# A decoder trunk's last product: one fixed order for the weight steps of VectorE, other rooms for raw tiles, differences and x2, and output copied out by ScalarE

## The chip, the cores and the metric

The kernel runs on one core of one Trainium2 chip. The metric is the device time of one execution in microseconds (us); lower is better. Times are given as the median over several runs. A profiled execution gives the trace that is read here.

## The reference, cut to what matters

One layer of a decoder, 256 tokens, width 2048, all in f32. The part that the change touches is the end: a SwiGLU feed-forward network (FFN) and the residual.

```python
D_MODEL, SEQ, D_FF = 2048, 256, 5632

def swiglu(h, w_ffn_in, w_ffn_out):
    gate, up = jnp.split(h @ w_ffn_in, 2, axis=-1)
    return (jax.nn.silu(gate) * up) @ w_ffn_out

def reference(x, c, ...):
    ...
    x = x + gate1 * mixing_sublayer(h, ...)          # attention and linear attention branches
    h = rms_norm(x, norm2_gain[l]) * (1 + scale2) + shift2
    x = x + gate2 * swiglu(h, w_ffn_in[l], w_ffn_out[l])
    return x
```

## The kernel before, in words

**Tiles and halves.** The 256 tokens are two token tiles of 128. A weight matrix is cut into column blocks of 512 and, along the summed dimension, into chunks of 128. A *raw tile* is two chunks of one column block: 128 x 1024 f32, 512 KB, loaded by one DMA on SyncE's queue (SP), line 159. To multiply f32 exactly enough, each raw tile is taken apart by `halve`: ScalarE (ACT) casts it to the rounded type, `whi` (line 166), and VectorE (DVE) takes the rest, `wlo` = raw - `whi` (line 167). Activations are kept as two halves too. TensorE (PE) then does three matmuls for one product (`mm3`): high by high (line 170), activation's high by `wlo` (171), activation's low by `whi` (172). `whi` and `wlo` each have a ring of four rooms, so a cast can run at most four tiles ahead of TensorE.

**Rooms for raw tiles.** `raw_tile` goes round a ring: four rooms of the pool tag `raw`, and after them the tags named in `rooms["extra"]`, which are places that other data held earlier. In the FFN these are A4 and A8; in the last product H4 to H7. H0 to H3 and H4 to H7 hold the two halves of the FFN's input activation h2.

**Stages.** The FFN's input product has eleven column blocks of gate and of up. The first is plain. In the ten others (and in the last product) `paired` works on two column blocks at once: over the first `4 n` chunks the 2 x 2 arrangement of token tiles and column blocks is computed with seven products instead of eight, by sums of activations (prepared in `h2_sums` or `act_sums`) and differences of raw tiles. With r0 and r1 the two column blocks of one half of the chunks, r2 and r3 those of the other half, the differences are

- t1 = r1 - r0, t2 = r3 - t1, t3 = r3 - r1, t4 = r2 - t2,

made by VectorE in `differ` (line 1230). Each raw tile or difference that is used is then taken to halves and multiplied: r0, t1, t2, r2, t3 first (six matmuls each, `product`), and after them "rest" tiles of plain products (twelve matmuls each) by turns with r3 and t4. Two additions of VectorE (line 1252) put partial sums together. The FFN's blocks have n = 1, the last product has n = 2 (two of each difference). The differences live in A13 and A14 (FFN), and in A13, A14, H2, H3 (last product).

**The last product** has four column blocks of the output, `w_ffn_out`, in the order of n = 0 to 3. At n = 0 and n = 2 `paired` computes two of them nearly to their end (the first and the third pass); n = 1 and n = 3 finish the second one. `add_out` then multiplies the PSUM tile by gate2 (line 1343), adds x2, the residual (line 1345), and stores. x2 is loaded back from DRAM into A2, A3, A4, A8 (line 1331).

**What sets the order.** The program is written once through, and a scheduler orders the instructions of each engine. Work inside `prio()` counts as if it stood several thousand places earlier, so loads, casts, low halves and differences are taken as early as the scheduler's own reckoning lets them. `tc.issue_after(x)` makes it keep an instruction behind x. Until now the differences had no such tie: `state["split"]` held the last low half only and served the running sums of `gate2` (`mac`). On the chip each engine then works through its list in order. The PSUM pool `acc` has four banks, all taken by a pair.

After an up block, VectorE multiplies silu(gate) by up (line 1319, two steps), and TensorE transposes the result (line 1071) during a later block.

## Time and profile before

| what | value |
|---|---|
| median of 3 runs | 1624.76 us (1622.45 to 1627.54) |
| profiled execution | 1626.09 us, span of its instructions 1624.3 us |
| TensorE busy | 1592.4 us, 98% of the span |
| VectorE busy | 1242.4 us, 76% |
| ScalarE busy | 855.2 us, 53% |
| FFN's input product, blocks 2 to 11 | about 936 to 1369 us of the span |
| last product | from 1369 us |
| mean granted clock of TensorE | 0.995 |

How to read the rows: a timeline row has the start in us, the duration in us, the engine, the line, the operation, output<-input by the program's names without buffer numbers, partitions x elements and type, and the count of merged instructions; in brackets the idle time of that engine before the row and what ended it. A row of a stretch has its bounds, its length, the busy time of PE, weight loads, DVE, ACT and POOL with their counts, the granted clock (1.00 is full), the busy share of the DMA engines, and GB/s. A row of the DMA list has output<-input, queue, operation, count, size, and the median us from issue to landing. TensorE's matmul records overlap, since a matmul starts before the one ahead has drained; the distance of two starts is what one costs.

### The profile page before, as it was taken

The page shows a single profiled execution, that of the slowest core. Times are in us where ns is not written, and L with a number is a line of the kernel's source. Part 1 is how long each engine was busy: PE and PEld are TensorE (multiplying, and loading weights), DVE is VectorE, ACT ScalarE, POOL GpSimd, SP SyncE. Part 2 cuts the span into 40 slices and gives each one's busy share as a digit, 9 for nine tenths or more (in the row PEclk, how much of TensorE's full clock was granted, in tenths as well). Part 3 has the DMA queues.
Part 4 walks back from the last instruction along what each step waited for, and adds up shares of the span by engine and source line. Part 5 has one row for each costly group of instructions (what it writes and reads, how often), then busy time and mean ns, then how long its engine had stood idle before and what let it go on. Part 6 is the DMA issues. An engine that isn't in the chain of part 4 may idle for free.

```text
span 1624.3 us, 20044 instructions
## 1 busy us (share of the span) xinstructions
PE 1592.4 (98%) x7269; PEld 1311.2 (81%) x7269; DVE 1242.4 (76%) x1418; ACT 855.2 (53%) x1180; POOL 5.4 (0%) x14
## 2 busy tenths in 40 slices
PE   8999999999999999999999999999999998999999
PEld 7878888788777888888887888888888886788787
DVE  6889995877779787878657788888888875755754
ACT  5654449756587444444445555555555553534432
POOL 1000000000000000000000000000000000000000
PEclk9999999999999999999999999999999999999999
DMA  8999997874767888888776577777776666665653
GB/s 325 354 326 323 325 312 224 281 267 136 249 231 233 265 305 311 314 289 314 236 219 226 161 252 253 259 254 252 245 232 194 185 190 224 206 200 178 211 154 114
DMA packets 116179, 399.24 MB, mean 246 GB/s; under 512 B 13090, under 2 KB 13896, under 8 KB 116080
## 3 DMA queue, kind: packets, MB, share of 16 engines
q1 hardware_dynamic: 115856, 397.95, 74.0%
q8 instruction: 57, 0.93, 0.2%
q14 instruction: 42, 0.34, 0.1%
q0 software_dynamic: 224, 0.01, 0.0%
HBM read 393.71 MB, written 4.19 MB: 245 GB/s over the span
## 4 chain that ended last, share of the span: by engine, by line
PE 89%; DVE 4%; DMA 3%; ACT 2%; issue 1%; POOL 0%; DVEq 0%; ACTq 0%; POOLq 0%
PE acc L172 27%; PE acc L171 27%; PE acc L170 27%; DVE wlo L167 2%; ACT whi L166 1%; PE misc L1071 1%; DMA H<-w_ffn_out 1%; PE acc L430 1%; DMA AR<-ada_rest 1%; PE misc L786 1%; DMA raw<-w_ffn_out 1%; PE misc L170 1%; PE misc L171 1%; PE misc L172 1%; DMA raw<-w_in 0%
## 5 line engine op out<-in xcount | busy, mean ns | idle before, releaser
L166 ACT CAST whi<-raw 128x1024 fp32r<-128x1024 f32 (+1 forms) x449 | 459.4, 1028 | 483.1 <-PE acc L172 365.0
L167 DVE TENSOR_TENSOR wlo<-raw,whi 128x1024 fp32r<-128x1024 f32 (+1 forms) x449 | 531.1, 1191 | 223.0 <-ACT whi L166 219.2
L170 PE MATMUL acc<-whi,H 128*128 128x512 f32 x1476 | 578.7, 392 | 0.8 <-ACT H L442 0.4
L171 PE MATMUL acc<-wlo,H 128*128 128x512 f32 x1476 | 578.0, 392 | 1.1 <-DVE wlo L167 1.0
L172 PE MATMUL acc<-whi,H 128*128 128x512 f32 x1476 | 578.1, 392 | 1.0 <-DVE H L1157 0.6
L172 PEld LDWEIGHTS acc<-whi,H 128*128 128x128 f32 x1476 | 278.1, 189 | 59.8 <-DVE H L449 1.8
L170 PEld LDWEIGHTS acc<-whi,H 128*128 128x128 f32 x1476 | 278.1, 188 | 58.3 <-ACT H L442 1.3
L171 PEld LDWEIGHTS acc<-wlo,H 128*128 128x128 f32 x1476 | 278.1, 188 | 58.0 <-DVE wlo L167 2.2
L166 ACT CAST whi<-A 128x1024 fp32r<-128x1024 f32 x98 | 103.0, 1054 | 89.1 <-PE acc L172 85.5
L167 DVE TENSOR_TENSOR wlo<-A,whi 128x1024 fp32r<-128x1024 f32 x98 | 118.7, 1221 | 30.8 <-ACT whi L166 29.9
L170 PE MATMUL acc<-whi,A 128*128 128x512 f32 x332 | 130.5, 393 | 6.7 <-ACT whi L166 6.7
L171 PE MATMUL acc<-wlo,A 128*128 128x512 f32 x332 | 129.8, 391 | 0.0
L172 PE MATMUL acc<-whi,A 128*128 128x512 f32 x312 | 122.0, 391 | 0.0
L287 DVE SCALAR_TENSOR_TENSOR ada<-AR,csil,ada 128x1024 f32<-128x1024 f32 x59 | 75.1, 1279 | 6.8 <-DMA AR<-ada_rest 6.8
L170 PEld LDWEIGHTS acc<-whi,A 128*128 128x128 f32 x332 | 62.6, 188 | 20.6 <-ACT whi L166 7.7
L166 ACT CAST whi<-H 128x1024 fp32r<-128x1024 f32 x41 | 43.0, 1053 | 63.7 <-PE acc L172 40.4
L167 DVE TENSOR_TENSOR wlo<-H,whi 128x1024 fp32r<-128x1024 f32 x41 | 49.9, 1223 | 34.2 <-ACT whi L166 29.2
L171 PEld LDWEIGHTS acc<-wlo,A 128*128 128x128 f32 x332 | 62.6, 188 | 13.4 <-DVE wlo L167 0.4
L172 PEld LDWEIGHTS acc<-whi,A 128*128 128x128 f32 x312 | 58.8, 189 | 12.1
L170 PE MATMUL acc<-whi,T 128*128 128x512 f32 x120 | 46.8, 390 | 0.0
L172 PE MATMUL acc<-whi,T 128*128 128x512 f32 x120 | 46.7, 389 | 0.0
L171 PE MATMUL acc<-wlo,T 128*128 128x512 f32 x120 | 46.7, 389 | 0.0
(402 smaller groups left out, 1556.7 us busy)
## 6 DMA issues: line engine op xcount, KB each, us to landing
raw<-w_in SPq DMA_DIRECT2D x203, 512.0 KB, 4.9
raw<-w_ffn_in SPq DMA_DIRECT2D x122, 512.0 KB, 4.5
AR<-ada_rest SPq DMA_DIRECT2D x79, 512.0 KB, 4.8
A<-w_ffn_in SPq DMA_DIRECT2D x54, 512.0 KB, 4.4
raw<-w_ffn_out SPq DMA_DIRECT2D x53, 512.0 KB, 4.3
H<-w_ffn_out SPq DMA_DIRECT2D x35, 512.0 KB, 4.5
raw<-w_out SPq DMA_DIRECT2D x32, 512.0 KB, 4.5
KC<-ada_rest SPq DMA_DIRECT2D x30, 512.0 KB, 5.3
```

The source lines that it names most:

```text
L166: nc.scalar.copy(hi, raw)
L167: state["split"] = nc.vector.tensor_tensor(lo, raw, hi.bitcast(F32), op=ALU.subtract)
L170: nc.tensor.matmul(ps, lh, rh, start=start, stop=False, skip_group_check=seeded)
L171: nc.tensor.matmul(ps, lh, rl, start=False, stop=False, skip_group_check=seeded)
L172: state["mm"] = nc.tensor.matmul(ps, ll, rh, start=False, stop=stop, skip_group_check=seeded)
L287: nc.vector.scalar_tensor_tensor(acc, raw, c, acc, op0=ALU.mult, op1=ALU.add)
L430: state["warm"] = nc.tensor.matmul(ps, ones_r, wide, start=True, stop=True)
L786: nc.tensor.matmul(ps[:n, t * N_GLA + h, :].rearrange("p (s l) -> p s l", l=L), at(f, h, t)[:, :n], odd(at(f, h, t)), start=True, stop=True,)
L1071: nc.tensor.transpose(ps[:, i, :], src[:, i * P : (i + 1) * P], ident)
```

## The change

1. `halve` and `differ` both go through a new `in_order`. Once `state["ordered"]` is set, each low half and each difference of VectorE is kept behind the one written ahead of it. The switch is set after the first column block of the FFN's input product (i = 0). `paired` writes its steps in another order: t1, r0, then t1's halves and t2 by turns, t2's halves, r2's halves and t3 by turns, t3's halves; t4 stands ahead of the rest tile that follows it. Raw tiles are asked for with all r0 first, then r1, r2, r3.
2. In the last product the extra rooms are A4 and A8, with H2 and H3 for the third pass; differences live in A13, A14, A2, A3; x2 in H4 to H7; the last tiles' halves in H2 to H5, A2, A3.
3. After the second and third pass (n = 1 and 2) ScalarE copies the two PSUM tiles to H4 (`kept`), and `add_out` reads the copy, without `prio()`.

```diff
--- before.py
+++ after.py
@@ -164,7 +164,12 @@
 
     def halve(hi, lo, raw):
         nc.scalar.copy(hi, raw)
-        state["split"] = nc.vector.tensor_tensor(lo, raw, hi.bitcast(F32), op=ALU.subtract)
+        state["split"] = in_order(lo, raw, hi.bitcast(F32), op=ALU.subtract)
+
+    def in_order(*args, **kw):
+
+        with tc.issue_after(state["split"].ins) if "ordered" in state else nullcontext():
+            return nc.vector.tensor_tensor(*args, **kw)
 
     def mm3(ps, lh, ll, rh, rl, start, stop, seeded=False):
         nc.tensor.matmul(ps, lh, rh, start=start, stop=False, skip_group_check=seeded)
@@ -1227,25 +1232,33 @@
 
         def differ(x, y, tag=None, into=None):
             d = S(tag, [P, 2, NB]) if into is None else into
-            nc.vector.tensor_tensor(d, x, y, op=ALU.subtract)
+            state["split"] = in_order(d, x, y, op=ALU.subtract)
             return d
 
         with prio():
-            raws = [(raw_tile(src, 4 * g, b0), raw_tile(src, 4 * g, b1)) for g in range(n)]
-            raws = [r + (raw_tile(src, 4 * g + 2, b0), raw_tile(src, 4 * g + 2, b1)) for g, r in enumerate(raws)]
+            raws = {(c, b, g): raw_tile(src, 4 * g + c, b) for c, b in ((0, b0), (0, b1), (2, b0), (2, b1)) for g in range(n)}
+            raws = [[raws[c, b, g] for c in (0, 2) for b in (b0, b1)] for g in range(n)]
+            t1 = [differ(r[1], r[0], p[0]) for p, r in zip(places, raws)]
             first = [halved(r[0]) for r in raws]
-            t1 = [differ(r[1], r[0], p[0]) for p, r in zip(places, raws)]
-            first += [halved(t) for t in t1]
-            t2 = [differ(r[3], t, p[1]) for p, r, t in zip(places, raws, t1)]
+            t2 = []
+            for p, r, t in zip(places, raws, t1):
+                first.append(halved(t))
+                t2.append(differ(r[3], t, p[1]))
             first += [halved(t) for t in t2]
-            first += [halved(r[2]) for r in raws]
-            first += [halved(differ(r[3], r[1], p[0])) for p, r in zip(places, raws)]
+            t3 = []
+            for p, r in zip(places, raws):
+                first.append(halved(r[2]))
+                t3.append(differ(r[3], r[1], p[0]))
+            first += [halved(t) for t in t3]
         rest = []
         for q in range(2 * n):
             g, k = q % n, 4 * n + 2 * q
+            if q < n:
+                with prio():
+                    differ(raws[g][2], t2[g], into=t2[g])
             w = load_weights(src, k, k + 2, b0)
             with prio():
-                rest.append((w, halved(raws[g][3] if q < n else differ(raws[g][2], t2[g], into=t2[g]))))
+                rest.append((w, halved(raws[g][3] if q < n else t2[g])))
 
         def add(dst):
             with prio(2 * AHEAD):
@@ -1310,6 +1323,7 @@
             block(pu, h2_at, w_ff, 0, KC, NFF)
             h2_sums = [left_sums(("A2", "A3"), ("A13", "A14"), h2[0][0], h2[1][0])]
             rooms["extra"] = ("A4", "A8")
+            state["ordered"] = True
         else:
             block(pu, h2_at, w_ff, 4, KC, NFF + i, go_on=True, seeded=True)
         hi = S(ftags[2 * i], [P, 4, T], F32R)
@@ -1324,10 +1338,9 @@
 
         later.append(turn)
         act.append((hi, lo))
-    rooms["extra"] = ()
     x2 = []
     for n in range(4):
-        xr = S(("A2", "A3", "A4", "A8")[n], [P, NT, NB])
+        xr = S(f"H{4 + n}", [P, NT, NB])
         nc.sync.dma_start(xr, x2_far[:, n])
         x2.append(xr)
 
@@ -1352,14 +1365,14 @@
     K0 = 4 * len(act_sums)
     for n in range(4):
         if n % 2 == 0:
-            rooms["extra"] = ("H4", "H5", "H6", "H7")
+            rooms["extra"] = ("A4", "A8", "H2", "H3")[: 2 + n]
             both = [[acc_bank() for _ in range(NT)] for _ in range(2)]
-            paired(act_at, act_sums, [("A13", "A14"), ("H2", "H3")], w_fo, n, n + 1, *both, KF)
+            paired(act_at, act_sums, [("A13", "A14"), ("A2", "A3")], w_fo, n, n + 1, *both, KF)
         pss = both[n % 2]
         if n == 3:
             rooms["extra"] = ()
             block(pss, act_at, w_fo, K0, CUT, n, more=True, go_on=True, seeded=True)
-            w = load_weights(w_fo, CUT, KF, n, spare=[f"H{j}" for j in range(2, 8)])
+            w = load_weights(w_fo, CUT, KF, n, spare=("H2", "H3", "H4", "H5", "A2", "A3"))
             block(pss, act_at, None, CUT, KF, 0, w=w, tiles=(0,), go_on=True, seeded=True)
             with prio():
                 add_out(n, 0, pss[0])
@@ -1381,9 +1394,16 @@
             if n == 0:
                 flush()
                 gate2 = state["gate2"]
+                with prio():
+                    for t in range(NT):
+                        add_out(n, t, pss[t])
+                continue
+            kept = S("H4", [P, NT, NB])
             with prio():
                 for t in range(NT):
-                    add_out(n, t, pss[t])
+                    nc.scalar.copy(kept[:, t, :], pss[t])
+            for t in range(NT):
+                add_out(n, t, kept[:, t, :])
 
 
 _INS = ["x", "c", "b_ada", "norm1_gain", "norm2_gain", "sb_q_gain", "sb_k_gain", "dil_q_gain", "dil_k_gain", "w_gla_a",
```

Line 167 (the low half) and 1230 (the difference) are both line 172 in the new text; 170 to 172 become 175 to 177, 1252 becomes 1265, 1319 becomes 1333, 1331 becomes 1344.

**VectorE in the first paired block of the FFN.** raw_1722 is r0, A4_1723 r1, A8_1724 r2, raw_1725 r3; A13 holds t1 and later t3, A14 t2 and later t4; raw_1739 is the first rest tile. Before:

```order
L167 TENSOR_TENSOR wlo_1727_8093<-raw_1722_8084,whi_1726_8092 128x1024
L167 TENSOR_TENSOR wlo_1730_8099<-A13_1728_8096,whi_1729_8098 128x1024
L1230 TENSOR_TENSOR A13_1736_8112<-raw_1725_8090,A4_1723_8086 128x1024
L167 TENSOR_TENSOR wlo_1733_8105<-A14_1731_8102,whi_1732_8104 128x1024
L1319 TENSOR_TENSOR scr_1680_7908<-scr_1680_7908,acc_1678_7906 128x512
L1319 TENSOR_TENSOR scr_1681_7910<-scr_1681_7910,acc_1679_7907 128x512
L1230 TENSOR_TENSOR A14_1731_8102<-A8_1724_8088,A14_1731_8102 128x1024
L167 TENSOR_TENSOR wlo_1735_8109<-A8_1724_8088,whi_1734_8108 128x1024
L167 TENSOR_TENSOR wlo_1738_8115<-A13_1736_8112,whi_1737_8114 128x1024
L1252 TENSOR_TENSOR acc_1718_8080<-acc_1717_8079,scr_1721_8083 128x512
L167 TENSOR_TENSOR wlo_1741_8121<-raw_1739_8118,whi_1740_8120 128x1024
```

Now, from t1's low half to the same rest tile:

```order
L172 TENSOR_TENSOR wlo_1730_8099<-A13_1726_8092,whi_1729_8098 128x1024
L172 TENSOR_TENSOR A14_1731_8102<-raw_1725_8090,A13_1726_8092 128x1024
L172 TENSOR_TENSOR wlo_1733_8105<-A14_1731_8102,whi_1732_8104 128x1024
L1333 TENSOR_TENSOR scr_1680_7908<-scr_1680_7908,acc_1678_7906 128x512
L1333 TENSOR_TENSOR scr_1681_7910<-scr_1681_7910,acc_1679_7907 128x512
L172 TENSOR_TENSOR wlo_1735_8109<-A8_1724_8088,whi_1734_8108 128x1024
L172 TENSOR_TENSOR A13_1736_8112<-raw_1725_8090,A4_1723_8086 128x1024
L1265 TENSOR_TENSOR acc_1718_8080<-acc_1717_8079,scr_1721_8083 128x512
L172 TENSOR_TENSOR wlo_1738_8115<-A13_1736_8112,whi_1737_8114 128x1024
L172 TENSOR_TENSOR A14_1731_8102<-A8_1724_8088,A14_1731_8102 128x1024
L172 TENSOR_TENSOR wlo_1741_8122<-raw_1739_8119,whi_1740_8121 128x1024
```

t2 (A14 from r3 and t1) was made further up and now stands behind t1's low half; t3 (A13 from r3 and r1) moves from ahead of the pair of line 1319 to behind r2's low half; t4 moves from ahead of r2's low half to just ahead of the rest tile's. The same holds in all ten paired blocks of the FFN.

**TensorE in the same block.** acc_1717 takes t3's product, acc_1716 the rest tile's, acc_1718 r3's. Before, from the last matmul of r2:

```order
L172 MATMUL acc_1716_8078<-whi_1734_8108,H4_1610_7514 128x512
L170 MATMUL acc_1717_8079<-whi_1737_8114,A2_1710_8063 128x512
L171 MATMUL acc_1717_8079<-wlo_1738_8115,A2_1710_8063 128x512
L172 MATMUL acc_1717_8079<-whi_1737_8114,A3_1711_8064 128x512
L170 MATMUL acc_1717_8079<-whi_1737_8114,A2_1710_8063 128x512
L171 MATMUL acc_1717_8079<-wlo_1738_8115,A2_1710_8063 128x512
L172 MATMUL acc_1717_8079<-whi_1737_8114,A3_1711_8064 128x512
L170 MATMUL acc_1716_8078<-whi_1740_8120,H1_1607_7511 128x512
L171 MATMUL acc_1716_8078<-wlo_1741_8121,H1_1607_7511 128x512
```

Now:

```order
L177 MATMUL acc_1716_8078<-whi_1734_8108,H4_1610_7514 128x512
L175 MATMUL acc_1717_8079<-whi_1737_8114,A2_1710_8063 128x512
L175 MATMUL acc_1716_8078<-whi_1740_8121,H1_1607_7511 128x512
L176 MATMUL acc_1717_8079<-wlo_1738_8115,A2_1710_8063 128x512
L177 MATMUL acc_1717_8079<-whi_1737_8114,A3_1711_8064 128x512
L175 MATMUL acc_1717_8079<-whi_1737_8114,A2_1710_8063 128x512
L176 MATMUL acc_1717_8079<-wlo_1738_8115,A2_1710_8063 128x512
L177 MATMUL acc_1717_8079<-whi_1737_8114,A3_1711_8064 128x512
L175 MATMUL acc_1718_8080<-whi_1742_8125,A2_1710_8063 128x512
L176 MATMUL acc_1716_8078<-wlo_1741_8122,H1_1607_7511 128x512
```

A matmul of the rest tile's high half stands ahead of t3's low half, and one of r3's high half ahead of the rest tile's low half; the first use of the rest tile's low half, the last row of both, is one row later.

**SyncE's loads at the start of the last product.** raw_2454 is the last tile of the FFN. Before, H5_11594 is the first r0, H6_11596 its r1, raw_11600 to raw_11606 are the second r1, the first r2 and r3, and the second r2:

```order
L159 DMA raw_2454_11498<-w_ffn_in 128x1024
L159 DMA raw_2472_11600<-w_ffn_out 128x1024
L1331 DMA A3_2460_11582<-x2_far_6951 128x1024
L159 DMA raw_2473_11602<-w_ffn_out 128x1024
L159 DMA raw_2474_11604<-w_ffn_out 128x1024
L1331 DMA A4_2461_11584<-x2_far_6951 128x1024
L1331 DMA A8_2462_11586<-x2_far_6951 128x1024
L159 DMA H5_2469_11594<-w_ffn_out 128x1024
L159 DMA raw_2475_11606<-w_ffn_out 128x1024
L159 DMA H6_2470_11596<-w_ffn_out 128x1024
L159 DMA H5_2503_11662<-w_ffn_out 128x1024
```

Now, raw_11594 and raw_11596 are the two r0, raw_11598 and A4_11600 the two r1, A8_11602 and raw_11604 the two r2, raw_11606 and raw_11608 the two r3:

```order
L159 DMA raw_2454_11498<-w_ffn_in 128x1024
L159 DMA raw_2469_11594<-w_ffn_out 128x1024
L159 DMA raw_2470_11596<-w_ffn_out 128x1024
L159 DMA raw_2471_11598<-w_ffn_out 128x1024
L159 DMA A4_2472_11600<-w_ffn_out 128x1024
L159 DMA A8_2473_11602<-w_ffn_out 128x1024
L1344 DMA H5_2460_11582<-x2_far_6951 128x1024
L159 DMA raw_2474_11604<-w_ffn_out 128x1024
L159 DMA H2_2637_12465<-w_ffn_out 128x1024
L159 DMA raw_2475_11606<-w_ffn_out 128x1024
L159 DMA raw_2476_11608<-w_ffn_out 128x1024
```

The first tiles' loads move from behind those of x2 and of other tiles to the place right behind the FFN's last load; H2_12465, a tile of the third pass, stands ahead of the two r3.

**VectorE at the start of the last product**, from the second step of the pair behind the last up block (line 1319, now 1333). Before:

```order
L1319 TENSOR_TENSOR scr_2438_11466<-scr_2438_11466,acc_2393_11247 128x512
L1230 TENSOR_TENSOR H2_2482_11620<-raw_2472_11600,H7_2471_11598 128x1024
L167 TENSOR_TENSOR wlo_2480_11615<-H7_2471_11598,whi_2479_11614 128x1024
L167 TENSOR_TENSOR wlo_2484_11623<-A13_2481_11618,whi_2483_11622 128x1024
L167 TENSOR_TENSOR wlo_2486_11627<-H2_2482_11620,whi_2485_11626 128x1024
L1230 TENSOR_TENSOR H3_2488_11632<-H4_2476_11608,H2_2482_11620 128x1024
L167 TENSOR_TENSOR wlo_2490_11635<-A14_2487_11630,whi_2489_11634 128x1024
L1230 TENSOR_TENSOR A13_2497_11650<-raw_2474_11604,H6_2470_11596 128x1024
L167 TENSOR_TENSOR wlo_2492_11639<-H3_2488_11632,whi_2491_11638 128x1024
L167 TENSOR_TENSOR wlo_2494_11643<-raw_2473_11602,whi_2493_11642 128x1024
```

Now:

```order
L1333 TENSOR_TENSOR scr_2438_11466<-scr_2438_11466,acc_2393_11247 128x512
L172 TENSOR_TENSOR A14_2485_11626<-raw_2475_11606,A13_2477_11610 128x1024
L172 TENSOR_TENSOR wlo_2487_11629<-A2_2478_11612,whi_2486_11628 128x1024
L172 TENSOR_TENSOR A3_2488_11632<-raw_2476_11608,A2_2478_11612 128x1024
L172 TENSOR_TENSOR wlo_2490_11635<-A14_2485_11626,whi_2489_11634 128x1024
L172 TENSOR_TENSOR wlo_2492_11639<-A3_2488_11632,whi_2491_11638 128x1024
L172 TENSOR_TENSOR wlo_2494_11643<-A8_2473_11602,whi_2493_11642 128x1024
L172 TENSOR_TENSOR A13_2495_11646<-raw_2475_11606,raw_2471_11598 128x1024
L1265 TENSOR_TENSOR acc_2465_11590<-acc_2464_11589,scr_2468_11593 128x512
L172 TENSOR_TENSOR wlo_2497_11649<-raw_2474_11604,whi_2496_11648 128x1024
L172 TENSOR_TENSOR A2_2498_11652<-raw_2476_11608,A4_2472_11600 128x1024
L172 TENSOR_TENSOR wlo_2500_11655<-A13_2495_11646,whi_2499_11654 128x1024
```

Low halves and differences come by turns in the order of the products; the addition into acc_2465 stands behind the first t3.

## The prediction

> **What bounds the kernel now.** First the page: shares of busy time, then the chain.
>
> ```profile
> span 1624.3 us, 20044 instructions
> PE 1592.4 (98%) x7269; PEld 1311.2 (81%) x7269; DVE 1242.4 (76%) x1418; ACT 855.2 (53%) x1180; POOL 5.4 (0%) x14
> PE 89%; DVE 4%; DMA 3%; ACT 2%; issue 1%; POOL 0%; DVEq 0%; ACTq 0%; POOLq 0%
> ```
>
> TensorE carries the end. Removed work elsewhere is worth nothing; only time in which TensorE waits can be gained or lost. Next the table by stretch (us; busy of PE, PEld, DVE, ACT, POOL; granted clock; DMA): up projections, first pass of the last product, its third pass, the rest.
>
> ```profile
> 890.00:1346.00 456.00, 456.00 (x2055) 377.55 (x2054) 374.12 (x380) 247.71 (x287) 0.00 (x0) 1.00 0.70 225
> 1369.20:1415.70 46.50, 39.19 (x157) 30.62 (x156) 37.22 (x34) 23.39 (x24) 0.00 (x0) 0.93 0.58 187
> 1500.00:1516.00 16.00, 12.99 (x51) 8.97 (x51) 16.00 (x18) 9.45 (x11) 0.00 (x0) 1.00 0.47 146
> 1516.00:1624.30 108.30, 104.36 (x471) 86.62 (x471) 54.81 (x53) 39.30 (x38) 0.00 (x0) 1.00 0.53 163
> ```
>
> In the FFN's input product (890 to 1346) TensorE never waits. A 512-wide matmul starts every 0.227 us (three rows below: 941.20 to 942.79 is seven). So 46.5 us hold 157 x 0.227 = 35.6 us of work: 10.9 lost in the first pass; the third loses 16.0 - 51 x 0.227 = 4.4. Both together, 15.3 us or 0.9%, are all there is to win.
>
> ```profile
> 1369.23 0.39 PE L170 MATMUL acc<-whi,A 128*128 128x512 f32 x1
> 1370.36 0.39 PE L172 MATMUL acc<-whi,A 128*128 128x512 f32 x1
> 1376.50 0.79 PE L170 MATMUL acc<-whi,A 128*128 128x512 f32 x1 [5.75 <-ACT whi L166]
> 1390.87 0.50 PE L170 MATMUL acc<-whi,AR 128*128 128x512 f32 x1 [0.52 <-ACT whi L166]
> 1375.40 1.04 ACT L166 CAST whi<-H 128x1024 fp32r<-128x1024 f32 x1 [8.49 <-DMA H<-w_ffn_out]
> 1380.00:1381.00 1.00, 1.00 (x3) 0.74 (x3) 1.00 (x1) 0.57 (x1) 0.00 (x0) 0.50 0.63 254
> 1381.00:1382.00 1.00, 1.00 (x4) 0.80 (x3) 1.00 (x2) 0.80 (x1) 0.00 (x0) 0.68 0.00 0
> ```
>
> The first product runs six matmuls at 1369.23 and then waits 5.75 us for a cast of a raw tile in an H room; H rooms hold the FFN's activation until that instant, so the load starts only then. The clock then stands at 0.50 (last two rows; 0.79 us for a matmul of 0.39) until about 1381.6: 5.1 us at half speed, 2.6 lost.
>
> **The change part by part.** *Loads (SP).* The first raw tiles of the last product go to raw, A4 and A8, which the FFN's own tiles leave one by one, so nothing of the first pair waits for the H rooms. The wait of 5.75 and the half clock after it go: the 10.9 us are freed, and what is late next is VectorE (below). SP now issues a load into H2 (for the third pass) that is held until H2 is read out, two tiles of 2.72 before 1369.23: 1363.8. The load of r3 stands behind it. Its own room comes free later still: VectorE ends the FFN (next row), then come two differences and r0's low half: 1359.63 + 3 x 1.14 + 1.22 = 1364.3. So being behind H2 costs nothing. With the load time of the second row, r3 is there at 1368.6; it is read at 1370.1 (below). The 1.5 us between are the cover; if they go, TensorE stops for as long as the load is late.
>
> ```profile
> 1359.63 1.23 DVE L167 TENSOR_TENSOR wlo<-raw,whi 128x1024 fp32r<-128x1024 f32 x1 [1.50 <-ACT whi L166]
> raw<-w_ffn_out SPq DMA_DIRECT2D x53, 512.0 KB, 4.3
> ```
>
> The Trainium skill ("TensorE: Matmul & The Clock Gate", Part 1) says that the clock halves after an idle window of about 3.4 us and is back after as much work; the trace agrees on the fall (5.75 us idle) and shows 5.1 us where the page has 3.4. By the page the clock part would be an estimated 1.7 us instead of 2.6, and what this step frees 10.0 instead of 10.9.
>
> *Copies by ScalarE, x2, places.* After the second and the third pass ScalarE copies two PSUM tiles each, and VectorE then multiplies and adds from the copy.
>
> ```profile
> 937.32 0.57 ACT L1268 COPY acc<-acc 128x512 f32<-128x512 f32 x1 [0.30 <-PE acc L172]
> 1498.45 1.06 ACT L166 CAST whi<-H 128x1024 fp32r<-128x1024 f32 x1 [1.67 <-PE acc L172]
> ```
>
> Four copies of 0.57, where ScalarE idles 1.67 before a cast (second row, at the start of the third pass): hidden by that idle time and 0 here; without it, 4 x 0.57 = 2.3. The banks that they empty are not the ones wanted next, so a gain there is 0 too. The other rooms for x2, differences and the last tiles change no count of instructions: 0, covered by rooms that were empty by then.
>
> *The fixed order of VectorE.* The switch is set after the FFN's first column block, so it also holds for the ten paired blocks of the FFN's input product. One of them before (ACT casts, VectorE, TensorE; E = 935.76 is where its products begin):
>
> ```profile
> 930.57 1.05 ACT L166 CAST whi<-A 128x1024 fp32r<-128x1024 f32 x1 [1.71 <-PE acc L172]
> 933.28 1.06 ACT L166 CAST whi<-A 128x1024 fp32r<-128x1024 f32 x1 [1.67 <-PE acc L172]
> 935.96 1.06 ACT L166 CAST whi<-A 128x1024 fp32r<-128x1024 f32 x1 [1.62 <-PE acc L172]
> 939.23 2.01 ACT L166 CAST whi<-raw 128x1024 fp32r<-128x1024 f32 x2
> 931.65 1.23 DVE L167 TENSOR_TENSOR wlo<-A,whi 128x1024 fp32r<-128x1024 f32 x1 [1.54 <-ACT whi L166]
> 932.91 1.22 DVE L1230 TENSOR_TENSOR A<-raw,A 128x1024 f32<-128x1024 f32 x1
> 934.37 1.23 DVE L167 TENSOR_TENSOR wlo<-A,whi 128x1024 fp32r<-128x1024 f32 x1 [0.24 <-ACT whi L166]
> 935.51 1.28 DVE L1319 TENSOR_TENSOR scr<-scr,acc 128x512 f32<-128x512 f32 x2
> 936.71 1.22 DVE L1230 TENSOR_TENSOR A<-A,A 128x1024 f32<-128x1024 f32 x1
> 937.85 2.35 DVE L167 TENSOR_TENSOR wlo<-A,whi 128x1024 fp32r<-128x1024 f32 x2
> 940.12 0.69 DVE L1252 TENSOR_TENSOR acc<-acc,scr 128x512 f32<-128x512 f32 x1
> 940.72 2.35 DVE L167 TENSOR_TENSOR wlo<-raw,whi 128x1024 fp32r<-128x1024 f32 x2
> 939.62 0.39 PE L172 MATMUL acc<-whi,A 128*128 128x512 f32 x1
> 941.20 0.39 PE L170 MATMUL acc<-whi,A 128*128 128x512 f32 x1
> 942.79 0.39 PE L171 MATMUL acc<-wlo,H 128*128 128x512 f32 x1
> ```
>
> The low half of the first "rest" tile is done at 940.72 + 1.22 = 941.94 and used at 942.79: 0.85 us of slack. VectorE steps follow each other in 1.14 us (936.71 to 937.85), a pair of L1319 in 1.20, L1252 in 0.60. ScalarE's casts follow in 0.95, and a cast starts 0.1 after the difference it reads:
>
> ```profile
> 1507.15 1.22 DVE L1230 TENSOR_TENSOR A<-H,raw 128x1024 f32<-128x1024 f32 x1
> 1508.48 1.05 ACT L166 CAST whi<-A 128x1024 fp32r<-128x1024 f32 x1 [1.59 <-DVE A L1230]
> ```
>
> In the new order t2's difference takes the place at 932.91 that t3's had. Then: difference done 934.13; cast 934.2 to 935.26 (0.93 later than before); low half of t2 935.3; the L1319 pair 936.44 to 937.64; low half of r2 937.64; t3's difference 938.78 to 940.0; addition 940.08 (its matmuls end at 939.62 + 0.39); t3's cast 940.1 to 941.16; t3's low half 941.2 to 942.42; t4's difference 942.34; first rest tile 943.45 to 944.67. TensorE now has two matmuls of other tiles ahead of that one and wants it at 941.20 + 8 x 0.227 = 943.01. It gets it at 944.72: 1.7 us lost in a block. Bounds: queued work alone (addition and cast waited for by nobody) ends 0.5 sooner, 1.2; with the slower first matmul after each wait (0.50 for 0.39 in the row of 1390.87) 1.9. Below 0 only if the order did not bind. I take 1.7, the walk over neighbouring rows. In the last two blocks eight transposes (0.8 us) stand ahead of that matmul and cover as much: 0.9. Sum: 8 x 1.7 + 2 x 0.9 = **+15.4** (10.4 to 17.4). What is queued behind on VectorE, the running sums for gate2 and the later low halves, has room again: tiles then run 2.72 us apart (930.57 to 933.28) against 1.14 of VectorE.
>
> *First pass, new.* TensorE wants the first rest tile after ten half tiles of six matmuls, at 1369.23 + 13.6 + 0.3 = 1383.1. VectorE ends the L1319 pair at about 1370.1 (its PSUM ends where the FFN does, at 1369.23 + 0.2, and the second step takes 0.6), then has five differences and eight low halves, 13 x 1.14, and one addition, 0.60: 1385.5. 2.4 lost, and 0.4 for slow starts: 2.8 (0 if the pair could go earlier, 5 if r3 is late). Term: -10.9 + 2.8 = **-8.1**.
>
> *Third pass.*
>
> ```profile
> 1500.97 0.39 PE L170 MATMUL misc<-whi,KC 128*128 128x512 f32 x1
> 1503.88 0.50 PE L171 MATMUL misc<-wlo,AR 128*128 128x512 f32 x1 [1.17 <-DVE wlo L167]
> 1513.58 0.49 PE L170 MATMUL acc<-whi,AR 128*128 128x512 f32 x1 [0.86 <-ACT whi L166]
> ```
>
> Its products begin 2.72 ahead of the first row, at 1498.25. The same 13 steps plus 0.60, and the output multiplications and additions of the second pass (four of 0.60, before and now: they move, but stand in this stretch still), from 1498.05 (t1's cast 2.48 ahead of the products, as at 933.28, then 1.06 and 1.22): 1515.9; TensorE wants 1512.2. 3.7 + 0.3 = 4.0 lost for 4.4 now: **-0.4** (-4 to +2).
>
> Sum: 15.4 - 8.1 - 0.4 = **+6.9**. Against the profiled execution (1626.09, of which 1.8 outside the span): 1633.0. The runs shown have a median of 1624.76, 1.3 under it; against that, **1631.6**. A measurement of this kernel can tell about 0.3%, 4.9 us, from no change.
>
> **The rivals.**
> 1. *Faster: the FFN's order is hidden.* VectorE is busy only 374 of 456 us there, and the reordered steps are the same in number. If the rest tile is ready by 943.01 in each block, only the last product counts: 1624.8 - 8.5 = 1616. It decides at 0.85 us a block. Against it: the idle time lies ahead of E, the late steps behind it. 0.13.
> 2. *Within 0.3%: the term is smaller,* 0.5 to 1.2 a block, as when addition and cast cost nothing. At 1.2 (0.4 in the last two): 10.4 - 8.5 = +1.9, 1627. For it: the walk hangs on small steps one after the other. Against it: each of them has a row. 0.26.
> 3. *The loads are late.* If r3 or a rest tile lands 5 us late, half of the first pass's gain is given back: +12, 1637. For it: SP is one queue, and rooms come free only as VectorE reads them. The first rest tile's room is r1's, read by t3's difference at 1378.2; with 4.3 the tile is there at 1382.5 and its cast must start at 1383.3: 0.8 us of cover. Against it: that is still cover in every term of the walk. 0.10.
> 4. *The clock falls in the FFN too.* Two waits a block at half clock for 5.1 us would cost 2.6 more in each, +26: 1658. Against it: the third pass has four such waits and keeps 1.00. The Trainium skill (the same page, "A second HAM failure mode: psum-queue depth-cycling") tells of short idle times between groups that make the clock swing; the trace has not shown it. 0.02.
>
> My forecast has 0.49.
>
> **How the numbers follow.** Forecast alone: 1627 to 1636. The range 1619 to 1639 takes in it and rivals 2 and 3 and leaves out rivals 1 and 4 (0.15). Slower by over 0.3% (above 1629.6): 0.45 of the forecast, rivals 3 and 4: 0.57. Faster: 0.13. Within: 0.30.
>
> **What would show it.** Right: in the ten FFN blocks a wait of 0.5 to 0.8 us of TensorE for a cast and one of 0.7 to 1.0 us for a low half, some 15 us over 890 to 1346, with the clock at 1.00; no wait for H at the last product's start and no 0.50 there; first and third pass each some 3 to 4 us. Wrong: TensorE's FFN window still full (rival 1); a cast of the first pass released by a DMA (rival 3). The prediction fails first if t2's cast is not later.

## The result and the profile after

The changed kernel takes 1632.97 us (median of 8 runs, 1631.82 to 1635.91) against 1627.22 us for the kernel before on the same chip (8 runs, 1622.45 to 1629.21). The ratio is 1.0045, 95% interval 1.0031 to 1.0059: 5 to 10 us slower. It is the ratio of the means, 1633.60 and 1626.27 us, 7.3 us apart; the medians are 5.75 us apart. The profiled execution's page, its span and its shares of busy time:

```profile
span 1631.4 us, 20029 instructions
PE 1595.3 (98%) x7269; PEld 1307.3 (80%) x7269; DVE 1243.0 (76%) x1418; ACT 857.6 (53%) x1184; POOL 5.3 (0%) x14
```

The work is the same but for four more steps of ScalarE, the copies; the shares of busy time say nothing of the loss. The table of TensorE's waits does (who waits, for whom, total us, times, longest). The rows for casts and for low halves, first of the kernel before (its lines 170 and 171 are 175 and 176 now):

```profile
PE acc L170 <- ACT whi L166: 8.9, 7, 5.8
PE acc L171 <- DVE wlo L167: 1.0, 1, 1.0
```

and of the changed kernel, in which the one long wait is gone and many short ones stand:

```profile
PE acc L176 <- DVE wlo L172: 9.3, 15, 1.0
PE acc L175 <- ACT whi L166: 5.2, 12, 0.6
```

Each of the ten paired blocks of the FFN's input product has one wait of each kind. Six others stand in the last product (shown below), and one, the longest with 1.0 us, far ahead of the FFN, where the kernel before has it too. The table by stretch, for the FFN's input product, the first pass of the last product, and the third pass:

```profile
890.00:1353.00 463.00, 453.00 (x2018) 368.27 (x2017) 369.44 (x377) 243.30 (x283) 0.00 (x0) 1.00 0.66 215
1385.40:1423.90 38.50, 36.92 (x157) 28.84 (x156) 32.59 (x30) 21.52 (x22) 0.00 (x0) 1.00 0.70 231
1506.00:1526.00 20.00, 17.89 (x73) 12.98 (x72) 20.00 (x22) 13.02 (x15) 0.00 (x0) 1.00 0.40 125
```

The FFN, which had TensorE busy for all of its 456 us, is now idle for 10.0 of 463 us. The time lost there is larger, 16.6 us by the distance of the starts: a matmul's row lasts 0.39 us where the next could start after 0.227, and the first starts behind a wait are further apart. The first pass, which begins at 1385.43 here, takes 38.5 us for the 157 matmuls that took 46.5. No stretch here is below full clock. In the third pass VectorE is busy for 20.00 of 20 us: that is what sets its pace.

One FFN block, the first, with ScalarE, VectorE and TensorE:

```profile
933.63 1.05 ACT L166 CAST whi<-A 128x1024 fp32r<-128x1024 f32 x1 [2.50 <-DVE A L172]
939.49 1.06 ACT L166 CAST whi<-A 128x1024 fp32r<-128x1024 f32 x1 [0.71 <-DVE A L172]
940.45 2.94 ACT L166 CAST whi<-raw 128x1024 fp32r<-128x1024 f32 x3
932.31 1.22 DVE L172 TENSOR_TENSOR A<-raw,A 128x1024 f32<-128x1024 f32 x1
934.72 1.22 DVE L172 TENSOR_TENSOR wlo<-A,whi 128x1024 fp32r<-128x1024 f32 x1 [1.19 <-ACT whi L166]
938.19 1.22 DVE L172 TENSOR_TENSOR A<-raw,A 128x1024 f32<-128x1024 f32 x1
940.58 1.22 DVE L172 TENSOR_TENSOR wlo<-A,whi 128x1024 fp32r<-128x1024 f32 x1 [0.27 <-ACT whi L166]
941.73 1.22 DVE L172 TENSOR_TENSOR A<-A,A 128x1024 f32<-128x1024 f32 x1
942.86 1.22 DVE L172 TENSOR_TENSOR wlo<-raw,whi 128x1024 fp32r<-128x1024 f32 x1
940.72 0.39 PE L175 MATMUL acc<-whi,A 128*128 128x512 f32 x1
941.54 0.50 PE L175 MATMUL acc<-whi,H 128*128 128x512 f32 x1 [0.44 <-ACT whi L166]
943.13 0.40 PE L175 MATMUL acc<-whi,A 128*128 128x512 f32 x1
944.13 0.50 PE L176 MATMUL acc<-wlo,H 128*128 128x512 f32 x1 [0.61 <-DVE wlo L172]
```

Read it in order of time. t2's difference (932.31) ends at 933.53, and t2's cast starts 0.1 later; before, this cast waited for TensorE alone. t2's low half (934.72) follows, t3's difference stands at 938.19 where before, in its own execution, it had been done at 934.1 (the products begin 0.5 us later there), so t3's cast ends only at 940.55. The casts behind it are late with it: TensorE starts t3's first matmul at 940.72 and waits for the next tile's cast until 941.54 (0.82 between two starts, where 0.227 is the pace: 0.59 lost). The low half of the rest tile ends at 942.86 + 1.22 = 944.08; TensorE's last start ahead of it is 943.13, and it goes on at 944.13: 0.77 lost. With 0.1 more for each of the next starts the block loses 1.67 us. The same two waits stand in all ten blocks.

The waits left in the last product, of the first pass and of the third, in the same view:

```profile
1385.19 1.28 DVE L1333 TENSOR_TENSOR scr<-scr,acc 128x512 f32<-128x512 f32 x2
1401.16 1.22 DVE L172 TENSOR_TENSOR wlo<-raw,whi 128x1024 fp32r<-128x1024 f32 x1
1395.76 0.50 PE L175 MATMUL acc<-whi,KC 128*128 128x512 f32 x1 [0.30 <-ACT whi L166]
1398.60 0.50 PE L176 MATMUL acc<-wlo,KC 128*128 128x512 f32 x1 [0.82 <-DVE wlo L172]
1402.43 0.50 PE L176 MATMUL acc<-wlo,A 128*128 128x512 f32 x1 [0.38 <-DVE wlo L172]
1517.23 0.50 PE L175 MATMUL acc<-whi,KC 128*128 128x512 f32 x1 [0.59 <-ACT whi L166]
1520.08 0.51 PE L176 MATMUL acc<-wlo,KC 128*128 128x512 f32 x1 [0.84 <-DVE wlo L172]
1524.09 0.51 PE L176 MATMUL acc<-wlo,A 128*128 128x512 f32 x1 [0.61 <-DVE wlo L172]
```

Each pass waits once for t3's first cast, once for t3's first low half and once for the first rest tile's low half; no wait of TensorE is released by a load.

### The profile page after: what moved, and what is told of

Read it like the earlier page. It is cut to its first block, busy times and chain, and to the rows that moved or that the text cites. A ratio compares the mean times of both kernels' runs of the same rounds, so it can differ in the third digit from the quotient of the medians.

```text
span 1631.4 us, 20029 instructions
## 1 busy us (share of the span) xinstructions
PE 1595.3 (98%) x7269; PEld 1307.3 (80%) x7269; DVE 1243.0 (76%) x1418; ACT 857.6 (53%) x1184; POOL 5.3 (0%) x14
## 4 chain that ended last, share of the span: by engine, by line
PE 84%; DVE 7%; ACT 3%; DMA 3%; issue 2%; POOL 0%; ACTq 0%; SPq 0%; DVEq 0%; POOLq 0%
PE acc L176 26%; PE acc L177 26%; PE acc L175 25%; DVE wlo L172 3%; DVE A L172 2%; ACT whi L166 2%; DMA AR<-ada_rest 1%; PE misc L1076 1%; PE acc L435 1%; DVE ada L292 1%; PE misc L791 1%; PE misc L176 1%; PE misc L177 1%; PE misc L175 1%; DMA raw<-w_in 0%
## 5 line engine op out<-in xcount | busy, mean ns | idle before, releaser
L172 DVE TENSOR_TENSOR wlo<-raw,whi 128x1024 fp32r<-128x1024 f32 (+1 forms) x458 | 542.5, 1191 | 245.3 <-ACT whi L166 243.1
L166 ACT CAST whi<-raw 128x1024 fp32r<-128x1024 f32 (+1 forms) x458 | 468.2, 1027 | 494.3 <-PE acc L177 369.4
L172 DVE TENSOR_TENSOR wlo<-A,whi 128x1024 fp32r<-128x1024 f32 x124 | 150.9, 1222 | 72.6 <-ACT whi L166 71.9
L166 ACT CAST whi<-A 128x1024 fp32r<-128x1024 f32 x124 | 129.5, 1052 | 135.8 <-PE acc L177 89.9
L177 PE MATMUL acc<-whi,OS 128*128 128x512 f32 x112 | 43.6, 389 | 0.0
L172 DVE TENSOR_TENSOR A<-raw,A 128x1024 f32<-128x1024 f32 (+1 forms) x30 | 36.5, 1218 | 1.7 <-ACT A L166 1.7
```

Of the source, the lines that this page charges most:

```text
L166: nc.scalar.copy(hi, raw)
L172: return nc.vector.tensor_tensor(*args, **kw)
L177: state["mm"] = nc.tensor.matmul(ps, ll, rh, start=False, stop=stop, skip_group_check=seeded)
```

## The experiments

Times of a kernel against the kernel before are from runs on the same chip (before: 1625.68 us in the first four, 1627.82 us in the last three). Beside them stands what the traces give, in us: the time that TensorE lost in the FFN's ten blocks (matmul starts further apart than 0.227 us, less the 1.05 us of such small gaps that every kernel here shows), in the first pass and in the third, and the length from the first matmul on the first block's t1 to the end. This length leaves out all that lies ahead of the FFN, where the profiled executions differ by up to 6 us (934.2 to 940.2 us for that first matmul) with the same work. The ratios are again those of the means.

| kernel | FFN | first pass | third pass | length | ratio, 95% interval |
|---|---|---|---|---|---|
| before | 0 | 11.0 | 4.7 | 687.2 | 1 |
| after | 16.6 | 2.9 | 3.6 | 694.8 | 1.0045 [1.0031, 1.0059] |
| e1_last_only | 0 | 2.8 | 3.6 | 677.8 | 0.9944 [0.9929, 0.9959] |
| e2_ffn_only | 16.6 | 10.5 | 4.3 | 703.0 | 1.0100 [1.0082, 1.0118] |
| e3_hoisted | 0 | 2.7 | 3.6 | 677.8 | 0.9943 [0.9928, 0.9957] |
| e4_t4_late | 8.9 | 2.1 | 2.8 | 685.4 | 0.9996 [0.9985, 1.0007] |
| e5_rooms_only | 0 | 6.6 | 4.7 | 682.6 | 0.9949 [0.9935, 0.9962] |
| e6_no_copy | 0 | 2.8 | 4.2 | 678.4 | 0.9931 [0.9919, 0.9943] |
| e7_late_out | 0 | 2.2 | 2.0 | 675.7 | 0.9926 [0.9914, 0.9939] |

The differences of the lengths follow from the three columns to within 0.3 us (before to e1: 15.7 lost becomes 6.4, 9.3 less; the lengths differ by 9.4).

**e1_last_only: the tie set only where the last product begins.**

```diff
             rooms["extra"] = ("A4", "A8")
-            state["ordered"] = True
...
         act.append((hi, lo))
+    state["ordered"] = True
```

> The fixed order is set only where the last product begins; the FFN's paired blocks are scheduled as before. Theory (the tie costs 16.4 us in the ten FFN blocks, the rest of the change frees 8.0 in the first pass and 1.0 in the third): the FFN's stretch is full again, first pass loses 2.9, third 3.5, and the time is 9.0 us under the kernel before, a ratio of 0.9945. Rival (the FFN's loss comes with something else in the change, such as the written order without the tie or later loads): the FFN still loses some 16 us and the ratio stays near 1.0045.

1616.3 us, 0.9944. The FFN in the table by stretch:

```profile
890.00:1345.00 455.00, 455.00 (x2057) 376.74 (x2056) 374.34 (x380) 247.72 (x287) 0.00 (x0) 1.00 0.70 225
```

TensorE is busy for all of it again. Between this kernel and the changed one only the fixed order in the FFN differs, 17.0 us of length.

**e2_ffn_only: the kernel before, with the tie and the new written order in the FFN's blocks alone.**

```diff
         act.append((hi, lo))
+    rooms["extra"] = ()
+    del state["ordered"]
...
-            rooms["extra"] = ("A4", "A8", "H2", "H3")[: 2 + n]
+            rooms["extra"] = ("H4", "H5", "H6", "H7")
```

(and the places, x2, the last tiles' rooms, the output and the order of writing in the last product as before).

> The kernel before, with the tie and the new written order in the FFN's ten paired blocks alone; last product, rooms and output as before. Theory: 1.67 us lost in each of the first eight blocks and 1.45 in the last two, 16.4 us more than before, a ratio of 1.010; the wait of 5.75 us and the half clock at the last product's start are still there. Rival (it is not the tie): ratio 1.000.

1642.2 us, 1.0100, as expected. TensorE's waits in this kernel:

```profile
PE acc L175 <- ACT whi L166: 13.2, 17, 5.1
PE acc L176 <- DVE wlo L172: 6.8, 11, 1.0
```

They are the two waits of each block, the 5 us wait at the last product's start, and shorter ones of the kind that the kernel before also had. The two parts of the change act side by side: +16.6 in the FFN here, and about -9.4 in the last product in e1.

**e3_hoisted: the tie kept in the FFN, the steps written in another order there** (t1, r0's halves, t2, t1's halves, t3, t2's halves, t4, r2's halves, t3's halves).

```diff
+                t1 = differ(r1, r0, p[0])
+                first = [halved(r0)]
+                t2 = differ(r3, t1, p[1])
+                first.append(halved(t1))
+                t3 = differ(r3, r1, p[0])
+                first.append(halved(t2))
+                t4 = differ(r2, t2, into=t2)
+                first += [halved(r2), halved(t3)]
```

> The changed kernel with the tie kept everywhere, but in the FFN's blocks the steps are written t1, r0, t2, t1's low half, t3, t2's low half, t4, r2's low half, t3's low half. Theory (it is the place of t2, t3 and t4 in the order, not that there is a fixed order): no TensorE wait in the FFN, ratio 0.9945 as without the tie there. Rival (any fixed order holds VectorE up): the FFN still loses 10 us or more, ratio 1.001 to 1.0045.

1615.95 us, 0.9943, no wait in the FFN. In the FFN the tie by itself costs nothing; the place of the differences in it does. VectorE in the first block: the differences t2, t3 and t4, and the low halves of two raw tiles, the first of them that of the rest tile:

```profile
928.82 1.22 DVE L172 TENSOR_TENSOR A<-raw,A 128x1024 f32<-128x1024 f32 x1
931.70 1.22 DVE L172 TENSOR_TENSOR A<-raw,A 128x1024 f32<-128x1024 f32 x1
935.50 1.22 DVE L172 TENSOR_TENSOR A<-A,A 128x1024 f32<-128x1024 f32 x1
939.50 2.35 DVE L172 TENSOR_TENSOR wlo<-raw,whi 128x1024 fp32r<-128x1024 f32 x2
```

The block's products begin 0.7 us earlier in this execution than in the changed kernel's (its first matmul on t1 starts at 935.91 and not 936.63). Beyond that shift t2 is made 2.8 us earlier than there, t3 5.8 and t4 5.5, and the rest tile's low half is done 6.2 us behind the products' beginning, as before the change, where it was 8.8 in the changed kernel. Differences that are made early fill time in which VectorE would wait for casts.

**e4_t4_late: the changed kernel with t4 behind the rest tile's low half.**

```diff
+            w = load_weights(src, k, k + 2, b0)
             if q < n:
                 with prio():
                     differ(raws[g][2], t2[g], into=t2[g])
-            w = load_weights(src, k, k + 2, b0)
```

> The changed kernel with one step moved: t4 is written behind the low half of the rest tile that follows it, in the FFN and in the last product. Theory (queued steps of VectorE add up, 1.14 us each): the second wait of each FFN block (0.77 us and its slow start of 0.11) goes, the first (0.60 and 0.20) stays; 8.3 us less in the FFN and 1.5 in the last product, ratio 0.9985. Rival (the next step, r3's low half, is then late in its place and the sum stays): ratio 1.002 to 1.0045.

1625.37 us, 0.9996. In the trace the second wait of every block is gone but for a slow start, and the first is as it was:

```profile
945.15 0.50 PE L175 MATMUL acc<-whi,H 128*128 128x512 f32 x1 [0.44 <-ACT whi L166]
945.32 1.22 DVE L172 TENSOR_TENSOR wlo<-raw,whi 128x1024 fp32r<-128x1024 f32 x1
946.46 1.22 DVE L172 TENSOR_TENSOR A<-A,A 128x1024 f32<-128x1024 f32 x1
```

So the 1.67 of a block fall to 0.8 in the last two blocks and to 0.9 to 0.95 in the first eight, where a slow start of 0.1 to 0.15 stays at the place of the second wait: 7.7 us less over the FFN, where 8.3 were expected. The two waits are two costs: the one from t3's late cast, the other from t4's step of 1.14 us ahead of the rest tile. The expected ratio, 0.9985, stands at the edge of the measured interval; the length gives 1.8 us less than before, the runs 0.6 less with an interval of 1.8 to each side.

**e5_rooms_only: the kernel before with the second part of the change alone** (asking order, rooms, places, x2, last tiles), no tie, no copies.

```diff
-            rooms["extra"] = ("H4", "H5", "H6", "H7")
+            rooms["extra"] = ("A4", "A8", "H2", "H3")[: 2 + n]
...
-            paired(act_at, act_sums, [("A13", "A14"), ("H2", "H3")], w_fo, n, n + 1, *both, KF)
+            paired(act_at, act_sums, [("A13", "A14"), ("A2", "A3")], w_fo, n, n + 1, *both, KF)
```

> The kernel before with the second part of the change alone: the asking order of the raw tiles and the other rooms for raw tiles, differences, x2 and last tiles; no tie on VectorE, the old written order, no copies. My theory: the rooms alone end the wait for an H room and the half clock, and VectorE, free to be ordered by the scheduler, serves the first pass at about 3 us lost (10.9 before); the third pass stays between 3.5 and 4.4; no wait in the FFN: 0.9945 to 0.996 of before. Rival: without the tie the scheduler puts a difference that needs a late load ahead of low halves that could run, VectorE stands still behind that load, and 4 to 7 us of the first pass come back: 0.998 to 1.000.

1618.95 us, 0.9949: the theory's ratio, but by the trace only in part for its reason. The wait for an H room is gone. The first pass loses 6.6 us and not 3, and the rival's mechanism is there. VectorE, TensorE and two slices of the table by stretch (first pass, third pass):

```profile
1369.40 1.23 DVE L1230 TENSOR_TENSOR A<-raw,A 128x1024 f32<-128x1024 f32 x1 [4.31 <-DMA raw<-w_ffn_out]
1370.54 1.22 DVE L167 TENSOR_TENSOR wlo<-A,whi 128x1024 fp32r<-128x1024 f32 x1
1371.82 0.50 PE L171 MATMUL misc<-wlo,KC 128*128 128x512 f32 x1 [0.69 <-DVE wlo L167]
1375.28 0.66 PE L171 MATMUL misc<-wlo,AR 128*128 128x512 f32 x1 [1.81 <-DVE wlo L167]
1376.00:1377.00 1.00, 1.00 (x3) 0.74 (x3) 1.00 (x2) 0.17 (x1) 0.00 (x0) 0.50 0.00 0
1509.00:1510.00 1.00, 1.00 (x3) 0.76 (x3) 1.00 (x2) 0.13 (x1) 0.00 (x0) 0.50 0.98 336
```

Here the scheduler put a t2 ahead of t1's first low half (1370.54). Its raw tile was late, VectorE stood 4.31 us behind the load, and the low half behind it, whose cast had been done at 1366.55, came late for TensorE. t1's second low half stands further back and is late too. Waits of 0.85 and 1.97 us follow, and then 3.4 us of half clock. With the tie (e6_no_copy, the same but for the tie and the written order) the first pass loses 2.8: tie and written order together are worth 4.2 us in the last product by the lengths; no run sets them apart there. By the lengths e5 should be 4.6 us faster than before, the runs say 8.3 (6.2 to 10.6). Of the rest 1.1 us lie ahead of the FFN, whose products begin at 934.61 here and at 935.76 before, and the others between profiled executions and runs: the runs of the kernel before were 1.2 us longer on average than its profiled one, at a mean granted clock of 0.9935 and not 0.9947, and those of e5 1.6 us shorter, at 0.9960 and not 0.9955. The clock goes the right way in both; why it differs is open.

**e6_no_copy: e1 without the copies by ScalarE.**

```diff
-            kept = S("H4", [P, NT, NB])
             with prio():
                 for t in range(NT):
-                    nc.scalar.copy(kept[:, t, :], pss[t])
-            for t in range(NT):
-                add_out(n, t, kept[:, t, :])
+                    add_out(n, t, pss[t])
```

> The kernel with the tie set only where the last product begins, and without the copies of ScalarE (the output of the second and third pass multiplied and added straight from PSUM, as before). My theory (term of the prediction: copies 0): the same time as with the copies, 0.9945 of before within 0.001, third pass 3.5 us lost. Rival: the copies do matter, since with them the multiplications and additions lose their early place and VectorE has more room in the third pass; without them the third pass loses 4.5 to 6 us: 0.995 to 0.996.

1615.5 us, 0.9931 [0.9919, 0.9943]: the rival's 0.995 is outside, and so, narrowly, is the theory's 0.9945. The third pass loses 4.2 us, between the theory's 3.5 and the rival's 4.5. By the trace the copies bring 0.6 us: without them VectorE does the four output steps at once, ahead of t2's difference, and t2's first low half (1492.50) is late:

```profile
1486.69 1.28 DVE L1356 TENSOR_TENSOR scr<-ada,acc 128x512 f32<-128x512 f32 x2
1487.89 1.29 DVE L1358 TENSOR_TENSOR H<-H,scr 128x512 f32<-128x512 f32 x2
1492.50 2.48 DVE L172 TENSOR_TENSOR wlo<-A,whi 128x1024 fp32r<-128x1024 f32 x2
1493.77 0.50 PE L176 MATMUL acc<-wlo,KC 128*128 128x512 f32 x1 [0.60 <-DVE wlo L172]
```

That is a new wait (1.1 us with its slow start and a small one ahead of it), for which later waits shrink. The runs cannot tell 0.6 us.

**e7_late_out: e1 with two steps moved:** t4 as in e4, and the second pass's output multiplied and added behind the third pass's products (the last tiles' halves then lie in A13 and A14 in place of A2 and A3).

```diff
+            w = load_weights(src, k, k + 2, b0)
             if q < n:
                 with prio():
                     differ(raws[g][2], t2[g], into=t2[g])
-            w = load_weights(src, k, k + 2, b0)
...
-            kept = S("H4", [P, NT, NB])
+            kept = S(("H4", "A2")[n - 1], [P, NT, NB])
...
+            if n == 1:
+                held_out = kept
+                continue
+            for t in range(NT):
+                add_out(1, t, held_out[:, t, :])
```

> The kernel with the tie set only where the last product begins, with two more moves: t4 stands behind the low half of the rest tile, and the multiplications and additions of the second pass's output are written behind those of the third (ScalarE's copy of it kept in A2 until then). My theory: TensorE waits in both passes only because VectorE has more steps than time between the products' beginning and the first rest tile; one step less of 1.14 there takes the first pass from 2.8 to 2.1 us, and one step and three of the four output steps less (0.60 each) take the third from 3.5 to about 1: 0.9925 to 0.993 of before. Rival: another release (a cast, a load, the addition of line 1265) is as late as VectorE, and the time stays at 0.9945.

1615.19 us, 0.9926, the lowest ratio here. It is the expected one, but e6 has nearly the same on that chip without these moves, so the runs do not show their worth; the lengths do, with 2.7 us against e6. VectorE and TensorE in the third pass:

```profile
1500.04 1.22 DVE L172 TENSOR_TENSOR wlo<-A,whi 128x1024 fp32r<-128x1024 f32 x1
1502.91 1.22 DVE L172 TENSOR_TENSOR wlo<-raw,whi 128x1024 fp32r<-128x1024 f32 x1
1501.32 0.50 PE L176 MATMUL acc<-wlo,KC 128*128 128x512 f32 x1 [0.84 <-DVE wlo L172]
```

The wait for the rest tile is gone in both passes. What is left is the wait for t3's cast and for t3's first low half (1500.04), which hang on steps that were not moved: the third pass still loses 2.0 us where about 1 was expected.

## Why the prediction was right

The forecast was 1631.6 us, 1632.97 came, and the sum of +6.9 us against the profiled execution stands beside 7.6 in the lengths and 7.3 by the ratio. The mechanism held in each of the three terms, but the closeness of the sum is in part luck: the FFN cost 1.2 us more than forecast and the third pass gained 0.7 more.

- **Fixed order in the FFN, +15.4: 16.6 measured,** inside its bounds (10.4 to 17.4). The walk's first block holds row for row: t2's cast predicted at 934.2 with the products beginning at 935.76, found at 933.63 with them beginning at 935.27; the loss 1.7 predicted, 1.67 found. The two waits fit the sizes named beforehand (0.5 to 0.8 and 0.7 to 1.0) by the distance of the starts, 0.60 and 0.78; TensorE's idle time alone, 0.44 and 0.61, is below them. e1, e2 and e3 show that it is this term and what in it: the place of the differences and not the tie.
- **The step that was mis-sized** is the one for the last two blocks. "Eight transposes (0.8 us)" ahead of the rest tile were to leave 0.9 lost; 1.45 was. The transposes do not stand there: they run at 1317.71 and 1362.77, 13 to 14 us behind that matmul. The rows of TensorE between t3's matmuls and the second wait, in the changed kernel's ninth block (the tenth reads the same):

```profile
1302.86 0.28 PE L955 MATMUL misc<-T,ones_r 128*128 128x256 f32 x1
1302.98 0.28 PE L956 MATMUL misc<-T,ones_r 128*128 128x256 f32 x1
1303.86 0.50 PE L176 MATMUL acc<-wlo,H 128*128 128x512 f32 x1 [0.37 <-DVE wlo L172]
```

Two matmuls of gate2, 0.12 us each, stand there, and they cover 0.24 of the second wait; the first wait has no cover at all. For two blocks that is 1.1 of the 1.2 us between 15.4 and 16.6.
- **First pass, -8.1: measured 11.0 to 2.9, -8.1.** The wait for an H room and the half clock are gone, and VectorE is late next, as said: the pair of line 1333 ends 1.0 us behind the products' beginning (1385.43; 0.9 predicted). That the 2.8 us of the new loss came to 2.9 is in part luck. The rest tile's low half is done 17.0 behind the products' beginning (16.3 predicted), and 62 matmuls, 14.1 us, stand ahead of its use (13.9 predicted): that is the 2.9, and the slow starts, for which 0.4 was added, lie in it for the most part. Nor does all of it stand at the rest tile: t3's first cast and first low half hold TensorE up before. The 5.1 us at half speed of the old pass are the part in which TensorE had matmuls to run; the half clock itself lasted from 1374.82 to 1381.64, 6.83 us by the trace's record of the granted clock.
- **Third pass, -0.4: measured -1.1.** The rest tile's low half is done 17.6 us behind the products' beginning, as predicted. Of the 0.7 more gained, 0.3 lies in the kernel before, which lost 4.7 where 4.4 was read, and 0.4 in the changed one: 17.6 less the same 14.1 us of matmuls is 3.5, without anything to add for slow starts.
- **Copies, x2, places, 0:** e6 puts the copies at a gain of 0.6 by the trace, too small for the runs. What was not seen is that the rooms by themselves would have left 6.6 us in the first pass (e5): the tie with its written order was needed there.
- **The rivals.** The first (the FFN's order hidden) and the second (0.5 to 1.2 a block) fell with 1.67 a block. The third (late loads) fell for the fixed order: no wait of TensorE and no cast in the first pass is released by a DMA; e5 shows the mechanism where the order is free. The fourth (half clock in the FFN) fell: the granted clock is 1.00 throughout it.

## What to carry to other kernels

A fixed order on an in-order engine is neither good nor bad; what counts is whether each step stands where the engine would otherwise wait. Here the differences belonged ahead of the products' beginning, among waits for casts, and behind it TensorE paid 1.67 us a block for them. A switch that is set for one stage should be set where that stage begins: tie and written order together gained 4 us in the last product and lost 17 in the stage before it, where TensorE had not waited.

## What was not expected of the hardware

The clock of TensorE fell to 0.50 in e5 with no long wait: it fell behind two waits of 0.85 and 1.97 us within 4.3 us, and stayed there from 1375.5 to 1378.9. In the third pass of the same kernel three waits of 1.02, 0.72 and 0.71 us within 3 us did the same. In the changed kernel waits of 0.46, 0.34 and 0.99 us within 3.3 us did not (all by the distance of the starts). The Trainium skill ("TensorE: Matmul & The Clock Gate", Part 1) has the clock fall after an idle window of about 3.4 us; the fall without any idle time of that length does not agree with it, the 3.4 us at half speed do.

The kernel before has the same three waits in its third pass (1.02, 0.72 and 0.72 us, ending at 1513.58 to 1515.48), and its clock did not fall. What differs is where they lie in time. By the traces' records of the granted clock, all falls of one execution begin whole multiples of 3.413 us apart, in each of the nine executions profiled. In the step ahead of a fall TensorE was always idle for at least 51%, by its matmul records. e5's three waits lie in one step (51% idle); in the kernel before a step ends between them (39% idle, then less than 20%). Some steps with up to 55% idle passed without a fall, so the exact condition is not shown.

How long half clock lasts goes by the same steps: one or two of them, 3.41 or 6.83 us, in every stretch of half clock that ended ahead of an execution's last matmul. Ahead of the FFN's input product every kernel here has the same short stop of TensorE. The table by stretch, 888 to 892 and 892 to 896 us, first of the kernel before:

```profile
888.00:892.00 4.00, 4.00 (x13) 3.22 (x12) 2.15 (x5) 1.46 (x4) 0.00 (x0) 0.50 0.36 122
892.00:896.00 4.00, 4.00 (x15) 3.21 (x15) 3.75 (x8) 2.11 (x6) 0.00 (x0) 0.81 0.19 68
```

and of the changed one:

```profile
888.00:892.00 4.00, 4.00 (x14) 3.21 (x15) 2.77 (x7) 1.71 (x5) 0.00 (x0) 0.64 0.52 157
892.00:896.00 4.00, 4.00 (x20) 3.27 (x19) 4.00 (x7) 2.60 (x6) 0.00 (x0) 1.00 0.17 63
```

Half clock lasts from 886.7 to 893.5 in the one (two steps) and from 887.5 to 890.9 in the other (one step), though nothing of the change lies there. One step more at half speed costs an estimated 1.7 us at most (half of 3.41), so a us or two between two profiled executions can come from this alone.

The first matmul behind a wait is followed 0.34 us later by the next, not 0.227 (941.54 to 941.88 in the first block), and where the wait was for a cast the second is late by 0.09 too. In an FFN block these slow starts are 0.3 of the 1.67 us.
